# Softmax gradient of 8192 x 8192 logits on one core: loads handed to Pool's queue, stores to SP's

## The chip, the cores and the metric

The kernel runs on one core of a Trainium2 chip. The metric is the device time of one execution in microseconds (us), here the median of three runs. A profile of one execution goes with it; its span runs from the first to the last instruction.

Names used below: VectorE is DVE in the profile, ScalarE is ACT, GpSimd is POOL or Pool, SyncE is SP. SP computes nothing; it only issues transfers. An engine works through its own queue of instructions in order, and a DMA issue that waits for a semaphore holds up all that stands behind it on that engine.

## The reference

For each of the 8 x 1024 positions there are 8192 logits and one label. The output is the softmax of the logits, less 1 at the label (the gradient of the cross entropy):

```python
logits_max = np.max(logits, axis=-1, keepdims=True)
exp_logits = np.exp(logits - logits_max)
softmax = exp_logits / np.sum(exp_logits, axis=-1, keepdims=True)
one_hot[batch_idx, seq_idx, labels] = 1.0
return (softmax - one_hot).astype(np.float32)
```

Logits and output are float32, 268.4 MB each. The labels are int32.

## The kernel before, in words

The 8192 positions are cut into 64 "rows" t of 128 positions, one per partition; a row is 128 x 8192 float32, 4096 KB. Two rows make a block b, so there are 32 blocks (`B`), and row t is row `t % 2` of block `t // 2`. In DRAM a partition's two rows of a block lie side by side, 64 KB in all. The buffer `X` holds three blocks (`SLOTS`), and block b uses slot `b % 3`; all the work on a row is done in place.

`load(b)` (line 120) issues the loads of a block. The string `LOADS` gives each block a letter: "r" is two transfers, one for each row; "w" is one transfer of the whole block. Blocks 0 to 4 and 26 to 31 are "r", the 21 between are "w". A load waits for the stores of the block that had the slot before, three blocks back, where they cover the same rows; blocks 0 to 2 have no such wait, except that the second row of block 2 waits for `iota`, since its place holds a scratch value at the start. `store(t)` (line 132) issues the store of row t and waits until VectorE has finished it (`finished[t]`). All go through `run` (line 63), which is why the profile gives line 68 for nearly every instruction.

Before the change all loads are issued by SP and all stores by ACT, which also issues the labels' load. The order on each engine is the order in which the loop emits the instructions. For row t that is:

- ACT: exponential of row t with its sum (waits for the row's maximum)
- VectorE: reciprocal of the sum
- if row t+1 begins a block: `load((t + 1) // G)`, so block 1's loads are emitted at t = 1, block 2's at t = 3
- VectorE: maximum of row t+1 (waits for that row's load)
- `store(t - 1)`, from t = 1 on
- ACT: scaling of row t by the reciprocal
- VectorE: subtraction of the one-hot row, by comparing `iota` with the label (this finishes row t)

Block 0's loads and the maximum of row 0 stand ahead of the loop. The last row is scaled and finished in two halves. At the end one engine waits for the last three blocks' stores. Ahead of all this Pool makes `iota` and an identity, TensorE transposes the labels, and VectorE copies both to where they are used; this takes 13.7 us.

Of the kernel before, what the change touches and what calls it, by code (L numbers as in the profile page):

```python
# [9 lines left out]
SLOTS = 3  # L10


LOADS = "rrrrrwwwwwwwwwwwwwwwwwwwwwrrrrrr"
STORES = "rrrrrrrrrrrrrrrrrrrrrrrrrrrrrrrr"


@with_exitstack
def kernel(
# [6 lines left out]
    nc = tc.nc  # L25
# [30 lines left out]
    with tc.tile_critical():  # L56
        sem = tc.alloc_semaphore
        got = [[sem(f"got{i}{q}") for q in range(2)] for i in range(SLOTS)]
        put = [[sem(f"put{i}{q}") for q in range(2)] for i in range(SLOTS)]
        lab_got, dve, act, pe, pool = (sem(n) for n in ("lab_got", "dve", "act", "pe", "pool"))  # L60
        count = {}

        def run(engine, waits, counter, method, **operands):

            waits = list(dict.fromkeys(waits))
            for w in waits[:-1]:
                engine.wait_ge(*w)
            instruction = getattr(engine, method)(**operands)  # L68
            for w in waits[-1:]:
                instruction._wait_ge(*w)  # L70
            step = 16 if method == "dma_start" else 1
            instruction.then_inc(counter, step)
            count[counter.name] = count.get(counter.name, 0) + step
            return counter, count[counter.name]
# [3 lines left out]
        w = run(nc.gpsimd, [], pool, "memset", ap=ident[:], constant=0.0)  # L78
# [13 lines left out]
        for j in range(G):  # L92
            w = run(
                nc.tensor, [w_ident, w_lab], pe, "transpose",
                out=lab_ps[:, j, :], in_=lab_f[:, j, :], identity=ident[:],
            )
# [14 lines left out]
        def meets(a, b):  # L111

            sets = [[set(range(*d.indices(n))) for d, n in zip(p, (P, G))] for p in (a, b)]
            return all(x & y for x, y in zip(*sets))


        loaded, stored, finished = {}, {}, []
        last_made = [((every, slice(G - 1, G)), w_iota)]

        def load(b):  # L120
            loaded[b] = []
            before = stored.get(b - SLOTS, last_made if b == SLOTS - 1 else [])
            for q, piece in enumerate(PIECES[LOADS[b]]):
                ps, js = piece
                free = [w for other, w in before if meets(piece, other)]
                w = run(
                    nc.sync, free, got[b % SLOTS][q], "dma_start",
                    out=X[ps, b % SLOTS, js, :], in_=x_b[b, ps, js, :],
                )
                loaded[b].append((piece, w))  # L130

        def store(t):
            b, j = divmod(t, G)
            stored.setdefault(b, [])
            for q, piece in enumerate(PIECES[STORES[b]]):
                ps, js = piece
                if js.stop != j + 1:
                    continue
                w = run(
                    nc.scalar, [finished[t]], put[b % SLOTS][q], "dma_start",  # L140
                    out=o_b[b, ps, js, :], in_=X[ps, b % SLOTS, js, :],
                )
                stored[b].append((piece, w))
# [12 lines left out]


        load(0)
        w_max = row_max(0)
        for t in range(T):  # L160
            x = row(t)
            label = lab[:, t % G, t // G : t // G + 1]
            w = run(
                nc.scalar, [w_max], act, "activation",
                out=x, in_=x, func=Act.Exp, bias=m[:, t : t + 1], scale=1.0, accum_out=s[:, t : t + 1],
            )
            w_sum = run(nc.vector, [w], dve, "reciprocal", out=r[:, t : t + 1], in_=s[:, t : t + 1])
            if t + 1 < T:
                if (t + 1) % G == 0:
                    load((t + 1) // G)  # L170
                w_max = row_max(t + 1)
            if t > 0:
                store(t - 1)
# [10 lines left out]
            for c, w in zip(cols, scaled):  # L184
                w = run(
                    nc.vector, [w], dve, "scalar_tensor_tensor",
                    out=x[:, c], in0=iota[:, c], scalar=label, in1=x[:, c],
                    op0=Alu.is_equal, op1=Alu.subtract, reverse1=True,
                )
            finished.append(w)  # L190
        store(T - 1)
        for b in range(B - SLOTS, B):
            for _, w in stored[b]:
                nc.scalar.wait_ge(*w)


# [28 lines left out]
```

## Time and profile before

| | us |
|---|---|
| time, median of 3 runs | 1247.98 (1247.91 to 1248.11) |
| span of the profiled execution | 1245.7 |
| own time of the profiled execution | not listed beside its span; the median above is 2.3 over the span |
| VectorE busy | 1119.2 (90%) |
| ACT busy | 919.1 (74%) |
| Pool busy | 7.4 |
| VectorE idle for loads | 94.3 in 25 waits |
| ACT idle for row maxima / for reciprocals | 188.4 / 115.9 |
| transfers | 536.98 MB at a mean of 431 GB/s |
| issue to landing, median: store / "r" load / "w" load | 30.8 / 26.6 / 33.4 |

Queue q1 is SP's and carries the loads; q10 is ACT's and carries the stores and the labels. The DMA share in a view of windows is the mean over the core's 16 DMA engines. A packet counts where it starts, so a short window can show more than 1.00. "Issue to landing" runs from the issuing instruction to the semaphore's full count.

### The profile page before, as it was taken

What the parts mean: (1) busy time and instruction counts of PE and PEld (TensorE: products, weight loads), DVE (VectorE), ACT (ScalarE), POOL (GpSimd) and SP (SyncE); (2) the same over time, 40 slices, a digit from 0 to 9 for tenths busy, and PEclk for the clock granted to TensorE, in tenths of its full rate; (3) what the DMA queues carried; (4) which work ended last, traced back from release to release, by engine and by line L of the source; (5) the groups of instructions that cost most, each with busy time, mean ns of one, the idle gap of its engine ahead of it and who ended that gap; (6) DMA issues with size and microseconds to landing.
All of it is one profiled execution on the core that took longest, in us unless ns stands there. A gap on an engine that the chain in (4) does not pass through costs nothing.

```text
span 1245.7 us, 592 instructions
## 1 busy us (share of the span) xinstructions
PE 0.4 (0%) x2; PEld 0.3 (0%) x2; DVE 1119.2 (90%) x196; ACT 919.1 (74%) x194; POOL 7.4 (1%) x7
## 2 busy tenths in 40 slices
PE   0000000000000000000000000000000000000000
PEld 0000000000000000000000000000000000000000
DVE  5999998888988889888998888988889999999893
ACT  3888886778776787767877778777777788887772
POOL 2000000000000000000000000000000000000000
DMA  9999999999999999999999999999999999999998
GB/s 406 417 429 433 438 433 442 437 426 427 430 435 445 439 417 442 426 430 437 432 443 438 420 435 432 430 437 450 420 426 437 436 428 432 437 435 429 432 437 386
DMA packets 15460, 536.98 MB, mean 431 GB/s; under 512 B 1728, under 2 KB 1728, under 8 KB 1760
## 3 DMA queue, kind: packets, MB, share of 16 engines
q1 hardware_dynamic: 6192, 268.44, 50.0%
q10 hardware_dynamic: 9264, 268.51, 49.9%
q14 instruction: 4, 0.03, 0.0%
HBM read 268.50 MB, written 268.44 MB: 431 GB/s over the span
## 4 chain that ended last, share of the span: by engine, by line
DMA 59%; DVE 37%; another core or an unknown queue 2%; ACT 1%; DVEq 0%; issue 0%; PE 0%; SPq 0%; ACTq 0%
DMA X<-in_logits_dram 31%; DMA out_dram<-X 27%; DVE m L68 18%; DVE X L68 18%; ACT X L68 1%; DVE iota L68 0%; DVEq L56 0%; DMA lab_raw<-in_labels_dram 0%; DVE lab_f L68 0%; DVE r L68 0%; PE iota L68 0%; SPq L68 0%; ACTq L68 0%; DVE lab L68 0%
## 5 line engine op out<-in xcount | busy, mean ns | idle before, releaser
L68 DVE TENSOR_REDUCE m<-X 128x1 f32<-128x8192 f32 x64 | 555.2, 8675 | 94.3 <-DMA X<-in_logits_dram 94.3
L68 ACT ACTIVATE X<-X,m 128x8192 f32<-128x8192 f32 x64 | 455.9, 7123 | 188.4 <-DVE m L68 188.4
L68 DVE SCALAR_TENSOR_TENSOR X<-iota,lab,X 128x8192 f32<-128x8192 int16 (+1 forms) x65 | 559.7, 8612 | 4.1 <-ACT X L68 4.1
L68 ACT ACTIVATE X<-X,r 128x8192 f32<-128x8192 f32 (+1 forms) x65 | 456.0, 7017 | 115.9 <-DVE r L68 115.9
L68 DVE RECIPROCAL r<-s 128x1 f32<-128x1 f32 x64 | 9.9, 154 | 7.3 <-ACT X L68 7.3
L68 ACT ACTIVATION_READ_ACCUMULATOR X<-X,m 128x1 f32 x64 | 12.0, 187 | 0.0
L68 DVE CAST lab_f<-lab_raw 32x256 f32<-32x256 int32 x1 | 3.7, 3685 | 4.7 <-DMA lab_raw<-in_labels_dram 4.7
L68 POOL IOTA X<- 128x8192 int16 x1 | 6.9, 6944 | 0.0
L68 DVE TENSOR_SCALAR iota<-X 128x4096 int32<-128x4096 int32 x1 | 4.4, 4427 | 0.1
L68 ACT ACT_TABLE_LOAD x1 | 1.3, 1283 | 1.3 <-SPq L56 1.3
L68 DVE COPY lab<-iota 128x64 f32<-128x64 f32 x1 | 0.2, 225 | 0.5 <-PE iota L68 0.5
L68 PE MATMUL iota<-ident,lab_f 32*128 32x32 f32 x2 | 0.4, 300 | 8.5 <-DVE lab_f L68 8.5
L68 PEld LDWEIGHTS iota<-ident,lab_f 32*128 32x128 f32 x2 | 0.3, 196 | 8.4 <-DVE lab_f L68 8.4
L68 POOL TENSOR_SCALAR_AFFINE_SELECT ident<-ident 32x32 f32<-32x32 f32 x1 | 0.2, 204 | 0.1
L68 POOL MEMSET ident<- 32x32 f32 x1 | 0.1, 115 | 0.5 <-SPq L56 0.5
L209 POOL MEMSET const-bfloat16-1.0<- 128x1 bf16 x1 | 0.1, 107 | 0.0
L209 POOL MEMSET const-uint8-127<- 128x1 uint8 x1 | 0.1, 107 | 0.0
L209 POOL MEMSET const-float32-0.0<- 128x1 f32 x1 | 0.1, 104 | 0.2 <-issue 0.2
L209 POOL MEMSET const-float32-1.0<- 128x1 f32 x1 | 0.1, 104 | 0.0
## 6 DMA issues: line engine op xcount, KB each, us to landing
out_dram<-X ACTq DMA_DIRECT2D x64, 4096.0 KB, 30.8
X<-in_logits_dram SPq DMA_DIRECT2D x22, 4096.0 KB, 26.6
X<-in_logits_dram SPq DMA_DIRECT2D x21, 33.4
lab_raw<-in_labels_dram ACTq DMA_DIRECT2D x1, 64.0 KB, 3.8
```

The costliest lines, as they stand in the source:

```text
L68: instruction = getattr(engine, method)(**operands)
L209: nc = _bacc.Bacc("TRN2", target_bir_lowering=False, num_devices=1)
```

## The change

Loads from block 3 on are issued by Pool (`nc.gpsimd`) and count on semaphores of their own, `got_pool`; those of blocks 0 to 2 stay on SP. The stores are issued by SP, in the place of the program where ACT issued them, and the waits at the end stand on SP. ACT issues the labels' load alone. Sizes, shapes, waits and the order of the emission are as they were.

```diff
+SOLO = 3
...
         got = [[sem(f"got{i}{q}") for q in range(2)] for i in range(SLOTS)]
+        got_pool = [[sem(f"got_pool{i}{q}") for q in range(2)] for i in range(SLOTS)]
...
                 free = [w for other, w in before if meets(piece, other)]
+                late = b >= SOLO
                 w = run(
-                    nc.sync, free, got[b % SLOTS][q], "dma_start",
+                    nc.gpsimd if late else nc.sync, free, got_pool[b % SLOTS][q] if late else got[b % SLOTS][q], "dma_start",
                     out=X[ps, b % SLOTS, js, :], in_=x_b[b, ps, js, :],
                 )
...
                 w = run(
-                    nc.scalar, [finished[t]], put[b % SLOTS][q], "dma_start",
+                    nc.sync, [finished[t]], put[b % SLOTS][q], "dma_start",
                     out=o_b[b, ps, js, :], in_=X[ps, b % SLOTS, js, :],
                 )
...
             for _, w in stored[b]:
-                nc.scalar.wait_ge(*w)
+                nc.sync.wait_ge(*w)
```

## The prediction

> **What bounds the kernel now.** I began with the share of DMA time, since the program reads and writes every byte once. These are the page's DMA line over 40 slices, its two large queues (kind, packets, MB, share of 16 engines), and the windows view over nearly the whole span (length, busy time of five engines, clock, DMA share, GB/s).
>
> ```profile
> DMA  9999999999999999999999999999999999999998
> q1 hardware_dynamic: 6192, 268.44, 50.0%
> q10 hardware_dynamic: 9264, 268.51, 49.9%
> 1.90:1244.20 1242.30, 0.42 (x2) 0.28 (x2) 1119.16 (x196) 918.57 (x194) 6.35 (x1) 1.00 1.00 432
> ```
>
> From 1.9 us to 1244.2 us the DMA engines have a share of 1.00 at 432 GB/s: no idle time is left in them. VectorE is busy 1119 of 1245.7 us and waits 94.3 us for loads. So the transfers are the bound, and the rule for this change is simple: each microsecond in which the DMA engines have nothing to move is added to the time, and an edit on ACT, SP or VectorE that leaves them full is worth nothing. One row (4096 KB = 4.194 MB) takes 4.194 / 0.432 = 9.7 us of all engines.
>
> Next I read the start, where the order of the queues matters. First the windows view, then the timeline (start, length, engine, operation), SP's own line first.
>
> ```profile
> 1.50:2.00 0.50, 0.00 (x0) 0.00 (x0) 0.00 (x0) 0.50 (x1) 0.50 (x1) 1.00 0.10 29
> 2.00:2.50 0.50, 0.00 (x0) 0.00 (x0) 0.00 (x0) 0.50 (x1) 0.50 (x1) 1.00 2.59 758
> ```
> ```profile
> 0.96 13.06 SPq L68 DMA_DIRECT2D X<-in_logits_dram  x6
> ...
> 38.21 8.74 DVE L68 SCALAR_TENSOR_TENSOR X<-iota,lab,X 128x8192 f32<-128x8192 int16 x1
> 46.98 0.36 ACTq L68 DMA_DIRECT2D out_dram<-X  x1
> 64.29 0.34 ACTq L68 DMA_DIRECT2D out_dram<-X  x1
> 81.56 8.67 DVE L68 TENSOR_REDUCE m<-X 128x1 f32<-128x8192 f32 x1
> ```
>
> SP issues six row loads (blocks 0, 1 and 2) by 14 us, that is 58 us of transfer. Store 0 cannot be issued before 46.98 us, when VectorE has finished row 0, and store 1 not before 64.29. It is block 2's two loads that keep the engines full from about 41 us until the stores take over. The line at 81.56 is the maximum of row 4, the first row of block 2.
>
> For the price of one transfer on idle engines I took the view of the logits' tile up to 240 us:
>
> ```profile
> DMA to landing us min/median/max: 12.2/30.7/60.1
> ```
>
> The shortest, 12.2 us, is the first load: issued at 0.96, data from about 2.4 (1.4 us later), 9.7 us of data, and 1.1 us until its semaphore is seen. So issue and landing cost 2.5 us beyond the data.
>
> **The change, part by part.** *The order on SP.* The stores now stand in SP's queue in program order. Block 1's loads are emitted at t=1, just ahead of store 0; store 1 is emitted at t=2; block 2's loads only at t=3. So SP's order is: loads of blocks 0 and 1, store 0, store 1, both loads of block 2, store 2 and so on. The change in words puts the first three blocks' loads ahead of the stores; the code does that for two. Store 0 waits on SP for VectorE until 46.95, and store 1 until 64.26, and block 2's loads are queued behind both. Who waits for that: the DMA engines at once, and VectorE's maximum of row 4 later.
>
> First gap: four rows are 4 x 9.7 = 38.8 us of data from 2.4, so the engines run dry at 41.2. Store 0 is issued at 46.98 and moves data 1.4 later, at 48.4. Idle: 7.2 us.
>
> Second gap: store 0's data ends at 48.4 + 9.7 = 58.1. Row 6 (block 3, now Pool's first load) may start when store 0 has landed, 1.1 later at 59.2, and at SP's price its data starts at 60.6: a gap of 2.5 us. Pool issues no DMA in this trace, so its price is bounded. Below: were its issue free, the landing's 1.1 us would remain; hence no gain. Above: store 1 is issued at 64.29 whatever Pool does, its data starts at 65.7, and the gap ends there at 7.6. The nearest rows are SP's and ACT's DMA issues (0.33 to 0.62 us of the queue's time) and Pool's short instructions (0.1 to 0.2 us; its longest, the iota, 6.9 us). I take SP's 2.5 plus 1.0 for work done by Pool in place of a hardware queue: 3.5 us, the ends 1.1 and 7.6 kept for the range. (The Trainium skill, "DMA: Bandwidth & Descriptors", § Specifications, gives a first byte after about 1 us for Pool's path and 0.6 us for SP's; by that 0.4 the gap would be an estimated 2.9 and the time 0.6 us less. No row here shows either.)
>
> From 65.7 on, store 1 and row 6 share the engines; at 82 us rows 4, 5 and 7 and store 2 (finished at 81.5 as now) are all queued, 4 x 9.7 = 39 us of work. Row 4 lands near 93 to 97, where VectorE wants it at 81.56, so VectorE falls 11 to 15 us behind. This costs nothing on top: store 3 then comes at about 115, before the 39 us are used up, and VectorE's 94.3 us of waiting for loads later on shrink by what it lost.
>
> *Steady state.* Loads wait for stores as before, on Pool in place of SP, in the same order. The chain of waits and ACT's timeline show what covers Pool's extra microsecond:
>
> ```profile
> 133.53 26.18 DMA out_dram<-X
> 159.72 32.61 DMA X<-in_logits_dram
> ...
> 150.84 0.34 ACTq L68 DMA_DIRECT2D out_dram<-X  x1
> ```
>
> When the store of 133.53 lands at 159.71 and releases a load, the next store, issued at 150.84, is still queued with most of its 9.7 us. So a load issued some microseconds later leaves no idle engine: nothing. If that cover were gone, each of the 29 blocks that Pool loads would pay up to 3.5 us.
>
> *ACT and the stores' wait.* ACT loses 63 issues before its last scale (0.34 us each, 21 us), but it waits 188.4 us for row maxima and 115.9 us for reciprocals: nothing. SP's steady queue holds stores alone, each waiting for its row; behind it stands only the next store. The final waits move from ACT to SP: nothing. The labels' load keeps its place.
>
> *The end.* Two lines of the timeline:
>
> ```profile
> 1199.76 8.69 DVE L68 TENSOR_REDUCE m<-X 128x1 f32<-128x8192 f32 x1 [1.93 <-DMA X<-in_logits_dram]
> ...
> 1230.18 0.34 ACTq L68 DMA_DIRECT2D out_dram<-X  x1
> ```
>
> The last row's load has landed at 1199.76, the last store is issued 30.4 us later, and alone it would take 12.2 us: 1242.4. The engines are busy to 1244.2, so the last load can come about 2 us later relative to the rest before an idle gap opens. Pool's 1.0 fits under that; at its upper end (5 us more than SP) 3 us would show.
>
> *Sum.* 7.2 + 3.5 = 10.7 us of new idle time on a span of 1245.7: 1256.4. The page gives no own time of the profiled execution; the three runs' median, 1247.98, is 2.3 above its span, and I carry that over: 1258.7 us, 0.9% slower. By the ends the sum is 8.3 to 17.8 us, or 1256 to 1266.
>
> **Rivals.** *1: no gap at the start (not slower).* If SP had block 2's loads issued before store 0, as the change in words says, the six loads would cover the start as now, and row 6 would be released by a landing that is covered too. Place: SP's queue before 47 us. It decides at one point: are block 2's loads issued before 41 us? Then 1248 us, with at most 1 or 2 us from the end. For it speaks only the wording; against it, the emission order in the loop. 5%. Faster by over 2.5 us would also need faster packets, against a share of 1.00 at one steady rate now: 2%, within that 5.
>
> *2: VectorE holds up Pool's issues.* Then each load of Pool would start only when the running VectorE instruction ends, and these rows are long:
>
> ```profile
> L68 DVE TENSOR_REDUCE m<-X 128x1 f32<-128x8192 f32 x64 | 555.2, 8675 | 94.3 <-DMA X<-in_logits_dram 94.3
> L68 DVE SCALAR_TENSOR_TENSOR X<-iota,lab,X 128x8192 f32<-128x8192 int16 (+1 forms) x65 | 559.7, 8612 | 4.1 <-ACT X L68 4.1
> ```
>
> A wait of up to 8.7, on average 4.3 us, brings the second gap to its cap of 7.6 and takes 4.3 + 1.0 - 2 = 3 us at the end: 1248 + 7.2 + 7.6 + 3 = 1266. With every wait near 8.7 the cover of 9.7 is nearly used up and it would be 1280 or more. Against it: 8192 elements in 8.6 us is below one element per nanosecond, so neither row shows a doubled rate. (The Trainium skill, "SBUF — State Buffer", § Who interferes with whom, lets only VectorE's two-port modes lock Pool out of writing descriptors, and by that rule neither instruction does; no row here tests it.) 8%.
>
> *3: the engines share differently between Pool's queue and SP's.* Now a load packet is as large as a store packet or larger (43 and 29 KB on average by the queue lines). If Pool's loads came in much smaller packets, they would lose turns to the stores, and the last load would land when hardly a store is left. The end chain of 30.4 + 12.2 = 42.6 us then holds three stores (29.1), so 13.5 us are idle: 1258.7 + 13.5 = 1272; more if Pool's round trip shows in each block (half of 29 x 3.5 = 51 us). The tensors' shapes, the same as before, speak against it; that another unit writes these transfers speaks for it. 13%.
>
> **How the numbers follow.** The forecast has 74%, with a range of its own of 1256 to 1266; rival 1 5%, rival 2 8%, rival 3 13%. For 8 in 10 I go from 1255 to 1272: it leaves out rival 1, the upper half of rivals 2 and 3, and a little below the forecast. 0.2% is 2.5 us, about what a measurement here can tell from no change: only rival 1 lies within it.
>
> **What would show it.** Right: the windows view idle from 41 to 48 us and again for about 3.5 us at 58, and full from 66 on to the end; on SP's timeline two stores ahead of block 2's loads, these at about 65 us; VectorE waiting 11 to 15 us for row 4. Pool's queue with about 243 MB (29 of 32 blocks), in packets of 32 and 64 KB. Wrong: six loads before store 0 (rival 1); idle slices in every block or loads that wait for VectorE's ends (rival 2); small packets, or a gap before the last store (rival 3).

## The result, and the profile after

The changed kernel takes 1265.87 us (median of four runs, 1264.6 to 1268.41) against 1247.97: a ratio of 1.0147, 95% interval 1.0132 to 1.0161. It is 17.9 us slower, where 10.7 was forecast. The profiled execution is the slowest of the four (1268.41 us, span 1266.6). Times here and below are medians; one execution of e8 was in a slower state (1286.55 us) and is left out.

The page's DMA line and queues (kind, packets, MB, share of 16 engines), and the windows view over nearly the whole span:

```profile
DMA  9799999999999999999999999999999999999996
q1 hardware_dynamic: 10080, 293.61, 53.8%
q0 software_dynamic: 5328, 243.27, 44.8%
1.90:1262.00 1260.10, 0.42 (x2) 0.28 (x2) 1116.57 (x196) 918.45 (x194) 26.01 (x38) 1.00 0.99 426
```

The same bytes move at 426 instead of 432 GB/s, and only the second and the last of the 40 slices show a dip. Pool's queue (q0) carries 243.27 MB in 5328 packets, 45.7 KB on average: data packets of 32 and 64 KB, as SP's were before. The start, as timeline and windows (length, busy time of five engines, clock, DMA share, GB/s):

```profile
0.96 1.90 SPq L70 DMA_DIRECT2D X<-in_logits_dram  x4
...
47.08 17.65 SPq L70 DMA_DIRECT2D out_dram<-X  x2
...
58.46 0.67 POOL L70 DMA_DIRECT2D X<-in_logits_dram  x1 [50.20 <-DMA out_dram<-X]
...
64.77 0.97 SPq L70 DMA_DIRECT2D X<-in_logits_dram  x2
...
97.90 8.69 DVE L70 TENSOR_REDUCE m<-X 128x1 f32<-128x8192 f32 x1 [16.17 <-DMA X<-in_logits_dram]
```
```profile
41.00:48.00 7.00, 0.00 (x0) 0.00 (x0) 7.00 (x3) 5.49 (x3) 0.00 (x0) 1.00 0.13 56
48.00:58.00 10.00, 0.00 (x0) 0.00 (x0) 10.00 (x2) 8.54 (x2) 0.00 (x0) 1.00 0.89 383
58.00:60.00 2.00, 0.00 (x0) 0.00 (x0) 2.00 (x1) 2.00 (x1) 0.67 (x1) 1.00 0.42 115
60.00:66.00 6.00, 0.00 (x0) 0.00 (x0) 6.00 (x3) 4.49 (x3) 0.00 (x0) 1.00 0.97 399
66.00:72.00 6.00, 0.00 (x0) 0.00 (x0) 6.00 (x1) 5.58 (x1) 0.00 (x0) 1.00 0.97 339
```

SP's order is the forecast one: four loads, two stores, and block 2's loads only at 64.77. The timeline's last line is the maximum of row 4, which waited 16.17 us for its load. The DMA engines are nearly idle from 41 to 48 us and again around 58 to 60. The last window holds something else: full engines (0.97) that move only 339 GB/s, where Pool's first load and store 1 run together. The packets take longer there: in the trace a 32 KB packet of Pool's load takes 1.6 us on average, against 1.2 in the kernel before. The same stretch in three views, from 40 to 72 us, of before, of the changed kernel and of e1_block2_first below:

```profile
40.00:72.00 32.00, 0.00 (x0) 0.00 (x0) 32.00 (x6) 27.00 (x6) 0.00 (x0) 1.00 1.02 423
...
40.00:72.00 32.00, 0.00 (x0) 0.00 (x0) 32.00 (x6) 27.09 (x6) 0.67 (x1) 1.00 0.73 293
...
40.00:72.00 32.00, 0.00 (x0) 0.00 (x0) 32.00 (x6) 27.00 (x6) 0.00 (x0) 1.00 1.01 426
```

By bytes, the start costs 32 x (1 - 293/423) = 9.8 us. I use this "start loss" for every kernel below, since it takes in idle engines and slow packets alike. A packet counts where it starts, so such a figure is good to about one microsecond. The end, in the windows view (the first line is the kernel before) and in SP's waits from 1200 us on (queue and line, what it waited for, us in total, times, longest):

```profile
1225.00:1240.00 15.00, 0.00 (x0) 0.00 (x0) 5.15 (x2) 0.00 (x0) 0.00 (x0) 1.00 1.02 439
...
1225.00:1240.00 15.00, 0.00 (x0) 0.00 (x0) 11.22 (x4) 11.02 (x4) 0.00 (x0) 1.00 0.93 402
1240.00:1250.00 10.00, 0.00 (x0) 0.00 (x0) 8.81 (x2) 3.51 (x1) 0.00 (x0) 1.00 0.76 328
```
```profile
SPq L197 <- DMA out_dram<-X: 13.0, 2, 9.6
SPq L57 <- POOLq L57: 2.4, 1, 2.4
```

Before the last store, which is issued at 1248.84, the engines are not full: the last load comes late relative to the rest. And when the last store has landed, SP still waits for Pool. At the end of the program each engine has an instruction called drain, and in the trace all of them wait for a semaphore that SP raises at 1262.50, after its last wait. Pool's drain then takes 3.09 us from 1262.54 on, those of the other engines 0.12 or less. The last data packet had ended at 1261.95. In the kernel before, 1.6 us lay between the last packet and the end of the span; here it is 4.7.

So 17.9 us = 9.8 at the start + 3.1 for the drain + 5.0 that is left. The first two are read from the profiled execution, which is 2.5 us over the median, so the 5.0 is rough. Part of what is left is idle engines before the last store: 15 x 0.07 + 10 x 0.24 = 3.5 us by the two windows above. Another part lies much earlier, between 130 and 200 us, here for before, the changed kernel, e7_gap_and_pool and e11_same_gap_no_pool:

```profile
130.00:200.00 70.00, 0.00 (x0) 0.00 (x0) 63.15 (x12) 52.23 (x12) 0.00 (x0) 1.00 1.00 432
...
130.00:200.00 70.00, 0.00 (x0) 0.00 (x0) 70.00 (x13) 58.10 (x13) 1.05 (x2) 1.00 1.00 422
...
130.00:200.00 70.00, 0.00 (x0) 0.00 (x0) 70.00 (x13) 58.10 (x13) 1.05 (x2) 1.00 0.96 406
...
130.00:200.00 70.00, 0.00 (x0) 0.00 (x0) 66.83 (x12) 58.10 (x13) 0.00 (x0) 1.00 1.00 433
```

By bytes the changed kernel loses 70 x (1 - 422/432) = 1.6 us here, and e7 loses 4.2. VectorE, behind since row 4, is busy throughout in both. The experiments take the three parts apart.

### The profile page after: what moved, and what is told of

It reads as the page before. It is cut to its first block, busy times and chain, and to the rows that moved or that the text cites. A ratio compares the mean times of both kernels' runs of the same rounds, so it can differ in the third digit from the quotient of the medians.

```text
span 1266.6 us, 592 instructions
## 1 busy us (share of the span) xinstructions
PE 0.4 (0%) x2; PEld 0.3 (0%) x2; DVE 1116.6 (88%) x196; ACT 919.0 (73%) x194; POOL 27.1 (2%) x44
## 3 DMA queue, kind: packets, MB, share of 16 engines
q0 software_dynamic: 5328, 243.27, 44.8%
## 4 chain that ended last, share of the span: by engine, by line
DMA 61%; DVE 35%; another core or an unknown queue 1%; ACT 1%; issue 0%; POOL 0%; PE 0%; SPq 0%; ACTq 0%; DVEq 0%
DMA X<-in_logits_dram 34%; DMA out_dram<-X 26%; DVE X L70 17%; DVE m L70 17%; ACT X L70 1%; DMA lab_raw<-in_labels_dram 1%; DVE iota L70 0%; DVE r L70 0%; DVE lab_f L70 0%; POOL X L70 0%; PE iota L70 0%; SPq L70 0%; DVE lab L70 0%; ACTq L223 0%
## 5 line engine op out<-in xcount | busy, mean ns | idle before, releaser
L70 POOL DMA_DIRECT2D X<-in_logits_dram x37 | 19.6, 531 | 1162.6 <-DMA out_dram<-X 1162.6
L70 DVE CAST lab_f<-lab_raw 32x256 f32<-32x256 int32 x1 | 0.8, 802 | 7.6 <-DMA lab_raw<-in_labels_dram 7.6
```

## The experiments

Each was measured beside the kernel before on its own chip (1247.53 to 1248.08 us).

**e1_block2_first, e2_pool_loads, e3_one_pool_block, e4_block2_late.** e1, against the changed kernel:

```diff
-                if (t + 1) % G == 0:
+                if (t + 1) % G == 0 and t + 1 != 2 * G:
                     load((t + 1) // G)
+                if t + 1 == G:
+                    load(2)
```

> The changed kernel, but SP issues block 2's two loads ahead of store 0 instead of behind store 1. Theory (the idle engines at 41 to 48 and 58 to 61 us come from that order and nothing else does): the windows view is full from 2 to 66 us, about 8 to 10 us less than the changed kernel, 1256 to 1258 us; Pool's last drain of 3.1 us and a gap of about 5 us before the last store stay, so it is still 8 to 10 us slower than before. Rival (Pool's queue as such is the cost): it stays within 3 us of the changed kernel, 1263 or more. Rival (the order was the only cost): 1248.

Measured: 1252.14 us, 4.1 over before, and below the theory's 1256 to 1258. The start loss is gone (426 GB/s above), which is the theory; but the time fell by 13.7, more than the start loss of 9.8. The gap before the last store, which the theory kept, went with it. The drain of 3.08 us stayed.

e2, against the changed kernel (stores and final waits back on ACT):

```diff
-                    nc.sync, [finished[t]], put[b % SLOTS][q], "dma_start",
+                    nc.scalar, [finished[t]], put[b % SLOTS][q], "dma_start",
...
-                nc.sync.wait_ge(*w)
+                nc.scalar.wait_ge(*w)
```

> The kernel before with the loads from block 3 on issued by Pool; the stores stay with ACT. No order on SP is changed. Theory: what is left is Pool's own price, the drain of 3.1 us plus a late last load (about 5 us) plus some slower packets: 1254 to 1258 us, equal to e1_block2_first within 2 us, since it does not matter whether SP or ACT issues the stores. Rival (the stores on SP cost or gain something): the two differ by more than 3 us.

Measured: 1249.17 us, ratio 1.0014 (1.0005 to 1.0024). Pool's queue by itself costs 1.1 us. The expectation, with a drain and a late load, was 5 us too high even at its lower end. Against e1 the time differs by 3.0, which e8 below puts down to the drain: in e2 it began at 1173.8 and ended at 1206.0, 1.6 us after Pool's last load had landed and long before the end.

e3, against e2:

```diff
-                late = b >= SOLO
+                late = b == SOLO
```

> The kernel before with block 3's two loads alone issued by Pool. Theory (the drain at the end is a fixed price of a program in which Pool has issued a DMA): 1247.98 + 3 = 1251 us, with a Pool drain of about 3.1 us as the last long piece. Rival (the drain grows with the number of Pool's DMAs or with how recent the last one is): 1248 to 1249 us with a drain below 1 us.

Measured: 1247.96 us, no difference. The theory of a fixed drain fell: with two DMAs of Pool the drain took 0.22 us, and lay at 1174 us besides. In the traces at hand it is 0.04 us for none, 0.22 for 2, 2.92 for 35 and 3.09 for 37, that is about 0.08 us for each DMA that Pool has issued (e2 and e7 aside, where the drain also holds the wait for Pool's last load).

e4, against the kernel before:

```diff
                 free = [w for other, w in before if meets(piece, other)]
+                if b == 2:
+                    free.append(finished[1])
```

> The kernel before (loads on SP, stores on ACT) with one wait more: block 2's loads wait until row 1 is finished (64.3 us). Block 3's loads stand behind them on SP. Theory (each idle microsecond of the DMA engines is added to the time): idle from 41.4 to 48.4 and from 58.1 to 65.7 us, 7 + 7.6 = 14.6 us, so 1262 to 1263 us, with no Pool DMA at all. Rival (part of an early gap is won back later): less than 1258.

Measured: 1264.0 us, 16.0 over before and 1 over the theory, with a start loss of 32 x (1 - 229/423) = 14.7 us and no Pool DMA. An early gap is not won back.

**e5_waits_on_act, e6_first_and_act, e7_gap_and_pool, e8_pool_waits_sp.** e5 is the changed kernel and e6 is e1, each with the final waits moved to ACT, which is one line:

```diff
-                nc.sync.wait_ge(*w)
+                nc.scalar.wait_ge(*w)
```

> The changed kernel, but the waits for the last three blocks' stores stand on ACT again instead of SP. Theory (the closing drain of Pool takes 3.09 us once Pool has issued DMAs, and it may begin only when SP has passed the end of its list; with the final waits on SP it comes after the last store, without them beside it): Pool's drain begins before the last store lands and the time falls by 3.1, from 1265.9 to about 1262.8 us. Rival (the drain follows the last landing anyway): no change, 1265 to 1266.

> Block 2's loads ahead of store 0 on SP, and the final waits on ACT; loads from block 3 on Pool and stores on SP as in the changed kernel. Theory (the order on SP and the place of the final waits are all that the change costs beyond Pool's small price): 1252.1 - 3.1 = 1249.0 us, the same as e2_pool_loads (1249.2), which has the stores on ACT. Rival (stores on SP have a price of their own): 1251 or more.

e8 is the reverse edit on e2, so the final waits stand on SP there:

> e2_pool_loads (loads from block 3 on Pool, stores on ACT) with the final waits on SP. Theory (the drain is put behind the last store by the waits on SP alone, whoever issues the stores): 3.1 us more than e2_pool_loads, 1252.3 us, with a Pool drain of 3.09 us near the end. Rival (it is the stores on SP that do it): 1249.2 as e2_pool_loads.

Measured: e5 1262.74 (3.1 less than the changed kernel), e6 1250.03 (2.1 less than e1), e8 1252.28 (3.1 more than e2). SP's late waits in e5 and in e8:

```profile
SPq L57 <- ACTq L57: 13.1, 1, 13.1
...
SPq L57 <- POOLq L57: 2.9, 1, 2.9
```

In e5 SP waits for ACT alone and Pool's drain (1247.6 to 1250.7) lies under the last store; in e8 SP waits 2.9 us for Pool after it. With the changed kernel and e2 these are all four pairings of stores and final waits on SP or ACT. This settles it: the place of the final waits decides whether the drain is paid for, whoever issues the stores, because Pool's drain waits until SP has come to the end of its list. e6 came out 1.0 above its expectation and within 0.9 of e2; a price of the stores on SP, if there is one, is no larger.

e7, against e2:

```diff
                 free = [w for other, w in before if meets(piece, other)]
+                if b == 2:
+                    free.append(finished[1])
```

> Stores on ACT, loads from block 3 on Pool, and block 2's loads on SP wait until row 1 is finished, so the start has the changed kernel's gaps. With before (no gap, no Pool), e4_block2_late (gap, no Pool: end as before) and e2_pool_loads (Pool, no gap) it makes a square. Theory (the gap at the start and Pool's queue together bring the loads' completions on the 16 engines apart and so the gap of about 5 us before the last store): 8.4 us at the start, about 3 for slow packets, 3 to 5 at the end, 1262 to 1265 us, last load's semaphores 4 us or more apart. Rival (the gap at the end needs the stores on SP): 1258 to 1260 us, the last load's semaphores within 3 us.

Measured: 1265.87 us, 0.9 over the theory's range, with a start loss of 9.7 (295 GB/s from 40 to 72 us) and its drain hidden, so 8.1 us are left over. What is left does not come from the stores on SP, since here they are on ACT. Half of it is lost between 130 and 200 us, as shown above; its engines fall to a share of 0.55 from 165 to 170 us.

**e9_second_gap_only, e10_pool_from_block4.** e9, against e5 (the new argument of `load` picks the row):

```diff
-                    load((t + 1) // G)
+                    load((t + 1) // G, (1,) if t + 1 == 2 * G else (0, 1))
+                if t + 1 == G:
+                    load(2, (0,))
```

> e5_waits_on_act, but row 4's load goes ahead of store 0 on SP and only row 5's stays behind store 1. The engines then stay full to about 61 us (five rows and store 0), and only the second gap is left, about 2.5 us near 61, after which Pool's first load still starts on idle engines. Theory (Pool's first load on idle engines sets the completions apart on the 16 engines and costs some 6 us more by slow packets and the gap at the end): 1248.0 + 2.5 + 6 = 1256 to 1258 us, with the gap before the last store at 3 us or more. Rival (the extra cost grows with the length of the gap at the start, or with how late VectorE gets): 1251 to 1253 us and an end as in e6_first_and_act.

e10, against e5:

```diff
-SOLO = 3
+SOLO = 4
...
-                if (t + 1) % G == 0:
+                if (t + 1) % G == 0 and t + 1 != 3 * G:
                     load((t + 1) // G)
+                if t + 1 == 2 * G:
+                    load(3)
```

> e5_waits_on_act, but block 3's two loads are issued by SP behind block 2's, so Pool starts with block 4, when the engines are full. The gaps at the start are those of e4_block2_late, 13.9 us. Theory (the extra cost needs Pool's load on idle engines): 1248.0 + 13.9 + 2 for slow packets + 1 to 2 for Pool's queue = 1265 to 1266 us, the end as in e2_pool_loads. Rival (any gap at the start together with Pool's queue later on brings it): 1248.0 + 13.9 + 6 to 9 = 1268 to 1271 us, with 3 us or more of idle engines before the last store.

Measured: e9 1254.47 us, 6.9 over before, of which 4.1 are start loss (369 GB/s) and 2.8 are left: between theory and rival, and its end was nearly full. e10 1264.3 us, 16.8 over before, 13.4 of it start loss (246 GB/s) and 3.4 left. Of these 1.9 are slow packets that reach past 72 us (419 GB/s from 72 to 130 us, against 433 before). The time is 0.7 under the theory's range and well under the rival's 1268.

**e11_same_gap_no_pool**, against the kernel before, with block 2's loads waiting for `finished[1]` as in e4, and:

```diff
+                if t + 1 == 2 * G:
+                    load(3, (0,))
                 if (t + 1) % G == 0:
-                    load((t + 1) // G)
+                    load((t + 1) // G, (1,) if t + 1 == 3 * G else (0, 1))
```

> The kernel before (all loads on SP, stores on ACT), with the changed kernel's order at the start: row 6's load as soon as store 0 has landed, then block 2's loads once row 1 is finished, then row 7's. The same two gaps as in the changed kernel (8.4 us), with no Pool DMA. Theory (the extra 6 us beyond gaps and drain need Pool's load on idle engines): 1248.0 + 8.4 + 2 = 1258 to 1259 us and 1 us of idle engines before the last store. Rival (the gaps and their order alone bring it): 1262 to 1265 us, with 3 us or more idle before the last store.

Measured: 1256.34 us, 8.4 over before, below the theory's 1258 to 1259. Its start and its end, as windows, against those of the changed kernel above:

```profile
40.00:72.00 32.00, 0.00 (x0) 0.00 (x0) 32.00 (x6) 26.99 (x6) 0.00 (x0) 1.00 0.77 311
...
1225.00:1240.00 15.00, 0.00 (x0) 0.00 (x0) 10.91 (x4) 10.12 (x4) 0.00 (x0) 1.00 0.98 424
1240.00:1250.00 10.00, 0.00 (x0) 0.00 (x0) 2.26 (x1) 0.00 (x0) 0.00 (x0) 1.00 0.95 406
```

The start loss is 32 x (1 - 311/423) = 8.5 us: all of the time, nothing left over. With the same order and no Pool DMA the engines stay full from 130 to 200 us and at the end. The gaps are not quite the same: the second is 1.6 us by the packets' records, against 2.4 in the changed kernel.

All kernels, in us over the kernel before beside them:

| kernel | loads from | gaps at start | total | start loss | drain at end | left |
|---|---|---|---|---|---|---|
| e4 | SP | both, longer | 16.0 | 14.7 | 0 | 1.3 |
| e11 | SP | both | 8.4 | 8.5 | 0 | -0.1 |
| e2 | Pool | none | 1.1 | 0 | 0 | 1.1 |
| e6 | Pool | none | 2.0 | 0 | 0 | 2.0 |
| e1 | Pool | none | 4.1 | 0 | 3.1 | 1.0 |
| e8 | Pool | none | 4.2 | 0 | 3.1 | 1.1 |
| e9 | Pool | second | 6.9 | 4.1 | 0 | 2.8 |
| e10 | Pool from block 4 | both, longer | 16.8 | 13.4 | 0 | 3.4 |
| e5 | Pool | both | 14.7 | 9.7 | 0 | 5.0 |
| e7 | Pool | both | 17.8 | 9.7 | 0 | 8.1 |
| changed | Pool | both | 17.9 | 9.8 | 3.1 | 5.0 |

What is left is 1.3 us or less without Pool's queue, 1.0 to 2.0 with it and full engines at the start, 2.8 and 3.4 with one gap or with Pool from block 4 on, and 5 to 8 when Pool's queue meets both gaps. The totals are medians, while start loss and drain come from one execution each, and the four executions of the changed kernel, of e5 and of e7 lie 4 to 5 us apart; so 5.0 and 8.1 do not differ clearly. In these runs neither the gaps alone (e4, e11) nor Pool's queue alone (e2, e6) brings it; it takes both. Not settled: how.

Two readings fit in part, and neither was tested alone. The first is VectorE's lateness. In the kernels with Pool's loads, what is left grows with the time at which VectorE starts row 5: 1.0 to 2.0 us at 99 (e1, e2, e6, e8), 2.8 and 3.4 at 103 (e9, and e10 with the 1.9 named above), 5.0 at 115 (e5 and the changed kernel), 8.1 at 118 (e7). Without Pool's loads e11 loses nothing at 110, but no kernel without them is as late as 115. The second is the spread of the 16 DMA engines. In the semaphore records the 16 increments of the last load come 1.3 us apart in before, 1.4 to 4.0 in e1, e2, e6 and e8, and 5.6, 4.1 and 5.1 in the changed kernel, e5 and e7, and a transfer counts as landed only with the last of them. But in e11 they are 4.0 apart with nothing lost. So the spread alone does not make the loss.

## Why the prediction was right, and where it was off

The direction and the main mechanism were right, and the time lies in the range; the forecast itself was 7.2 us too low. That the time lies within the narrower 1256 to 1266 as well is luck. That upper end stood for a Pool 5 us slower than SP, with a second gap of 7.6 us and 3 us at the end; but the gap was 2.4, and the place was filled by the drain and by losses that need no slow Pool.

- **The bound.** Right: the time follows the DMA engines' losses in e11 (8.5 lost, 8.4 measured) and within 1.3 us in e4 (14.7 lost, 16.0 measured).
- **Rival 1's deciding point and the wording of the change.** Block 2's loads did stand behind two stores. e1 moved them and 13.7 us went.
- **The two gaps.** Sized at 7.2 + 3.5 = 10.7; by bytes 9.8. The engines are idle for less, 5.9 and 2.4 us by the packets' records; slow packets after them make up the rest. What was mis-sized is SP's price, the 1.4 us from issue to data: in the changed kernel store 0's first packet starts 0.8 us after SP issued it. In e11 SP issues row 6 at 58.12 and its first packet starts 0.97 us later; in the changed kernel Pool issues it at 58.46 and its first packet starts 1.38 us later. The second gap is 1.6 us in e11 and 2.4 here, so the one microsecond for Pool over SP was about right, and the 2.5 under it too high. (The Trainium skill, "DMA: Bandwidth & Descriptors", § Specifications, puts 0.4 us between the two paths' first bytes; 1.38 against 0.97 us agrees.)
- **VectorE late by 11 to 15 us, at no cost.** It was 16.2 us, row 4 starting at 97.90. e11 starts row 4 at 92.86 and loses nothing by it, so 11 us cost nothing there. For the 16 us of the changed kernel this is not shown: from 130 to 200 us, with VectorE busy throughout, it loses 1.6 us and e7 4.2.
- **Steady state.** Right apart from the stretch up to 200 us: 433 GB/s from 200 us on to 1000, before and after, and e2 puts Pool's whole price at 1.1 us.
- **"The final waits move from ACT to SP: nothing".** Wrong by 3.1 us. I counted what is queued behind the waits in the loop, and not the closing sequence, in which Pool's drain stands behind SP. The drain is new too, as it grows with Pool's DMAs.
- **"Pool's 1.0 fits under that" slack of 2 us at the end.** Wrong for this kernel: about 3.5 us of idle engines lie there, of 5 that are left over. For Pool's queue without the gaps it was right (e2: 1.1 in all). The two terms were priced apart, and together they cost more than their sum.
- **Rivals 2 and 3.** Neither. Pool issued at 58.46 in 0.67 us, and its data flowed before 60, while VectorE was busy from 55.62 to 64.3 with one row's last step. (The rule of the Trainium skill, "SBUF — State Buffer", § Who interferes with whom, by which this step does not lock Pool out, agrees.) The packets kept their sizes. The gap before the last store, which the prediction named as a sign of rival 3 and priced at 13.5 us, did come, at about 3.5 us, but without rival 3's cause.

No version here beats the kernel before, whose DMA share is 1.00 from first to last packet.

## What to carry to other kernels

Where transfers fill the DMA engines, price a moved queue by the first microsecond at which the engines run dry: write down each queue's order as the loop emits it and find the first issue that waits for compute with loads behind it. Changing the engine that issues the loads cost 1.1 us here; the order on the queue that got the stores cost 9.8 at the start, and 13.7 with what followed from it. Then follow what comes after the last store: here the final waits on SP put 3.1 us of Pool's drain behind it.

## What was not expected of the hardware

Pool's closing drain grows with the DMAs that it has issued: 0.22 us for 2 and 3.09 for 37. Where a load and a store start within some microseconds on idle engines, the first packets take longer: 339 GB/s at a share of 0.97 from 66 to 72 us, and 388 at 1.00 in e11, without Pool. And where the engines ran dry at the start and Pool's queue carries the loads, 5 to 8 us more are lost later, part of it between 130 and 200 us (422 GB/s against 432) and part before the last store, more than 1100 us after the gaps; the cause is open.
